# A decoder layer's last stretch: LayerNorm statistics as row sums on ScalarE, another order of the last products, norms in pieces

## The chip, the cores and the metric

The kernel runs on one core of one Trainium2 chip. Five engines work side by side, each through its own queue in order: TensorE (PE in the profile), VectorE (DVE), ScalarE (ACT), GpSimd (POOL) and SyncE (SP), which starts the transfers. They wait for one another through semaphores. The metric is the time of one execution on the device in microseconds (us); lower is better.

## The reference, cut to what matters

One layer over 1024 positions of width 1024, in float32. The change lies in the last two steps: the rest of the down product with LN2, and the gated embedding with LN3.

```python
def layer_norm(x, g, b):
    mu = jnp.mean(xf, axis=-1, keepdims=True)
    var = jnp.mean(jnp.square(xf - mu), axis=-1, keepdims=True)
    y = (xf - mu) * lax.rsqrt(var + LN_EPS)
    return (y * g + b)
...
h = jnp.square(jax.nn.relu(x @ w_up[i])) @ w_down[i]
x = layer_norm(DN_ALPHA * x + h, ln2_g[i], ln2_b[i])
ple = (p[i] @ w_ple[i]) * jax.nn.sigmoid(x @ w_ple_gate[i])
x = layer_norm(DN_ALPHA * x + ple, ln3_g[i], ln3_b[i])
```

## The kernel before

The 1024 positions are eight tiles of 128 rows (`xres[0]` to `xres[7]`, 128x1024 each, in SBUF). Every matrix product is three matmuls (`mm3`, lines 69 to 71): each float32 operand is split into a rounded high part and the low rest, and high x high, high x low and low x high are added in PSUM. ScalarE makes high parts (casts), VectorE or GpSimd low parts (a subtraction).

The down product runs in stages over the hidden width; each stage forms seven products p1 to p7 of half-size blocks (the seven-product scheme of Strassen's kind), each for four tiles t. One call `down(s, name, t)` (line 902) is one block: six matmuls into a PSUM bank, and one addition on VectorE out of that bank (`into`, line 890). Two chains share banks: p1, p6, p7, p4 go on in one bank per t, and p3 goes on in the bank in which p5 began, so a later block of a chain can start only when the addition of the block before it has read the bank. By `takers`, p5 of t goes to the right half of `xres[4+t]`, p3 to the right half of `xres[t]`, p7 and p4 to the right and left halves of `xres[4+t]`. So p3 of t is the last that `xres[t]` gets, and p4 of t the last for `xres[4+t]`.

In the last stage (line 1210 on) the order is `SEQ`: twelve blocks of p1, p2 and p6, then p5, p3, p7 and p4, four each. Beside them the next phase is prepared. The gate matrix is loaded in eight row blocks k; ScalarE casts the high part of each (line 1168), GpSimd subtracts for the low part (`gate_rest`, line 1158, 128x1024 each). `norm2(i)` is LN2 of tile i on VectorE: two `bn_stats` of 512 columns, `bn_aggr`, the addition of epsilon, the power -1/2 on GpSimd (line 103), and two passes over 128x1024 (lines 110 and 113). `turn2(i)` transposes a normed tile on TensorE (two PSUM banks of tag b0) and casts it; `rest2` subtracts its low part on VectorE.

Then comes the gate phase, one turn per tile i (line 1235): `gate` is 24 matmuls for each half of the columns (banks of tags b4 and b6, which the down product used for t = 2, 3 and t = 0, 1), a sigmoid on ScalarE and a product with the embedding on GpSimd; between the halves `turn2(i+1)`; then on VectorE LN3 of tile i-1, `rest2(i+1)`, LN2 of tile i+2 and two `merge` additions. The last tile goes in four quarters with the product on VectorE, and ends with its own LN3 and store.

What sets the order: under `manual_schedule` the named engines take instructions as the code is written. In the tail these are TensorE and VectorE, and GpSimd in a part of it; ScalarE and SyncE are ordered by a planner.

## Time and profile before

| what | value |
|---|---|
| median of 3 runs | 1250.26 us (1249.97 to 1251.74) |
| the profiled execution | 1249.6 us, of which span 1247.8 us |
| TensorE busy / weight loads | 94% / 78% of the span |
| VectorE, ScalarE, GpSimd busy | 75%, 45%, 43% |
| mean granted TensorE clock | 0.973 of full |

The span runs from the first to the last instruction of the profiled execution; the rest of its time lies around it. A stretch of the profile is read by what TensorE does in it: whether it is busy, at which granted clock (1.00 is 2.4 GHz, 0.50 is 1.2 GHz), and which engine ended its waits. A matmul's printed duration includes its pipeline, so the pace of TensorE is read from start to start. In this profile the last stage's p5 blocks begin at 1105 us, the first gate product at 1136.7, and TensorE's last matmul ends near 1239.9.

### The profile page before, as it was taken

Reading aid. Unit: us, or ns where it says so; the run is one execution under the profiler, and the core shown is the slowest. Engines: PE = TensorE matmul, PEld = TensorE weight load, DVE = VectorE, ACT = ScalarE, POOL = GpSimd, SP = SyncE. Lnnn points to the kernel's source line nnn. Section 1 sums busy time; section 2 is a strip of 40 time slices with the busy share of each in tenths; the row PEclk is TensorE's granted clock in tenths of the full one; section 3 lists DMA queues with packets and bytes.
Section 4 is the critical chain, followed back from the end, with each engine's and each line's share of the span. In section 5 each row is a group of like instructions: output and inputs, shape, how many; then the busy total and the mean of one; then the engine's idle time right before and its main releaser. Section 6 shows DMA issues by size and latency. Waiting matters only on the chain.

```text
span 1247.8 us, 15501 instructions
## 1 busy us (share of the span) xinstructions
PE 1169.4 (94%) x5520; PEld 967.2 (78%) x5520; DVE 939.1 (75%) x1169; ACT 558.1 (45%) x948; POOL 533.1 (43%) x368
## 2 busy tenths in 40 slices
PE   7999998899987998799899999999999999998997
PEld 5877777788866877688688888878888888876876
DVE  7745868796854678887577777688887888876998
ACT  5425756575644244455354554555433243421111
POOL 3212444454651336642334324257644456472432
PEclk9999999999997998899899999999999999998999
DMA  9824112121236373387788878899555665431121
GB/s 348 294 104 135 32 54 60 43 59 60 71 87 232 113 256 107 109 281 259 258 270 259 283 246 264 275 409 393 198 170 187 214 208 193 145 130 74 68 85 68
DMA packets 123580, 221.48 MB, mean 177 GB/s; under 512 B 9456, under 2 KB 64240, under 8 KB 123504
## 3 DMA queue, kind: packets, MB, share of 16 engines
q1 hardware_dynamic: 123504, 220.50, 52.3%
q8 instruction: 43, 0.70, 0.2%
q14 instruction: 33, 0.27, 0.1%
HBM read 148.12 MB, written 70.25 MB: 175 GB/s over the span
## 4 chain that ended last, share of the span: by engine, by line
PE 67%; DVE 12%; DMA 6%; issue 5%; ACT 5%; POOL 4%; SPq 1%; DVEq 0%; POOLq 0%; ACTq 0%
PE pd L69 7%; PE pd L70 7%; PE pd L71 7%; PE pu L71 6%; PE pu L70 6%; PE pu L69 6%; PE tp L126 3%; PE pq L69 3%; PE pq L70 2%; PE pq L71 2%; PE acc L70 2%; PE acc L69 2%; PE o L429 2%; PE acc L71 2%; DVE rr L400 2%
## 5 line engine op out<-in xcount | busy, mean ns | idle before, releaser
L890 DVE TENSOR_TENSOR xres<-xres,pd 128x512 f32<-128x512 f32 x208 | 137.0, 682 | 47.2 <-PE pd L71 46.6
L574 POOL TENSOR_TENSOR draw<-draw 128x512 f32<-128x512 f32 x64 | 97.9, 1530 | 174.0 <-DMA draw<-in_w_down_dram 171.3
L574 POOL TENSOR_TENSOR dop<-draw,dop 128x1024 fp32r<-128x1024 f32 (+1 forms) x48 | 112.5, 2362 | 127.3 <-ACT dop L866 121.2
L866 ACT CAST dop<-draw 128x1024 fp32r<-128x1024 f32 (+1 forms) x96 | 81.1, 905 | 135.8 <-PE pd L71 46.5
L69 PE MATMUL pd<-dop 128*128 128x512 f32 x320 | 125.5, 392 | 0.8 <-DVE xres L890 0.7
L70 PE MATMUL pd<-dop 128*128 128x512 f32 x320 | 124.9, 390 | 0.0
L71 PE MATMUL pd<-dop 128*128 128x512 f32 x320 | 124.7, 390 | 0.0
L103 POOL TENSOR_TENSOR rs<-var,mhalf 128x1 f32<-128x1 f32 x32 | 43.9, 1375 | 102.5 <-DVE var L101 95.9
L574 DVE TENSOR_TENSOR dop<-draw,dop 128x1024 fp32r<-128x1024 f32 (+1 forms) x48 | 85.7, 1786 | 2.5 <-ACT dop L866 2.5
L751 ACT COPY hid<-pu 128x512 f32<-128x512 f32 x48 | 28.3, 589 | 120.6 <-PE pu L71 68.3
L69 PE MATMUL pq<-xh,wh 128*128 128x512 f32 x192 | 78.2, 407 | 0.8 <-DVE ul L66 0.8
L400 DVE TENSOR_TENSOR_SCAN rr<-rr,diag 128x640 f32<-128x640 f32 (+3 forms) x32 | 71.4, 2232 | 8.2 <-ACT rr L398 8.1
L71 PE MATMUL pq<-xh,wl 128*128 128x512 f32 x192 | 76.6, 399 | 0.0
L70 PE MATMUL pq<-xl,wh 128*128 128x512 f32 x192 | 76.5, 399 | 0.0
L403 POOL TENSOR_TENSOR aa<-aa,rr 128x639 f32<-128x639 f32 (+3 forms) x32 | 56.9, 1780 | 44.9 <-DVE rr L400 44.9
L69 PEld LDWEIGHTS pd<-dop 128*128 128x128 f32 x320 | 60.4, 189 | 14.9 <-DVE xres L890 1.1
L70 PEld LDWEIGHTS pd<-dop 128*128 128x128 f32 x320 | 60.3, 189 | 12.6 <-POOL dop L574 0.3
L71 PEld LDWEIGHTS pd<-dop 128*128 128x128 f32 x320 | 60.2, 188 | 12.6
L574 DVE TENSOR_TENSOR hid<-pu,hid 128x512 f32<-128x512 f32 x48 | 33.0, 688 | 44.8 <-PE pu L71 36.8
L66 DVE TENSOR_TENSOR atl<-tp,ath 128x512 fp32r<-128x512 f32 (+2 forms) x96 | 50.8, 547 | 14.7 <-ACT ath L65 14.0
L65 ACT CAST wh<-wraw 128x1024 fp32r<-128x1024 f32 x36 | 38.0, 1057 | 51.2 <-PE acc L70 24.9
L70 PE MATMUL acc<-wl,mix 128*128 128x512 f32 x128 | 52.8, 412 | 2.4 <-POOL wl L66 2.4
(244 smaller groups left out, 3378.3 us busy)
## 6 DMA issues: line engine op xcount, KB each, us to landing
hspill<-hid SPq DMA_DIRECT2D x48, 512.0 KB, 5.0
draw<-hspill SPq DMA_DIRECT2D x48, 512.0 KB, 6.1
uraw<-in_w_up_dram SPq DMA_DIRECT2D x32, 512.0 KB, 6.3
draw<-in_w_down_dram SPq DMA_DIRECT2D x32, 512.0 KB, 4.5
tspill<-draw SPq DMA_DIRECT2D x64, 256.0 KB, 4.4
wraw<-in_w_out_dram SPq DMA_DIRECT2D x24, 512.0 KB, 3.6
draw<-in_w_down_dram SPq DMA_DIRECT2D x48, 256.0 KB, 5.1
wraw<-in_w_in_dram SPq DMA_DIRECT2D x16, 512.0 KB, 4.9
```

Source lines behind the costliest of these rows:

```text
L65: A.copy(out=h, in_=src)
L66: (eng or V).tensor_tensor(out=l, in0=src, in1=h.bitcast(F32), op=ALU.subtract)
L69: T.matmul(ps, lhsT=lh, rhs=rh, start=start, stop=False, **kw)
L70: T.matmul(ps, lhsT=lh, rhs=rl, start=False, stop=False, **kw)
L71: T.matmul(ps, lhsT=ll, rhs=rh, start=False, stop=stop, **kw)
L103: G.tensor_tensor(out=rs, in0=var, in1=mhalf[:, 0:1], op=ALU.pow)
L126: T.transpose(tp[:, j * P:(j + 1) * P], src[:, (k0 + j) * P:(k0 + j + 1) * P], ident)
L400: V.tensor_tensor_scan(out=rr[:, 0:n][:, ::-1], data0=rr[:, 0:n][:, ::-1], data1=diag[:, S - n:S][:, ::-1], initial=0.0, op0=ALU.mult, op1 ...
L403: G.tensor_tensor(out=aa[:, 0:n - 1], in0=aa[:, 0:n - 1], in1=rr[:, 1:n], op=ALU.mult)
L574: eng.tensor_tensor(out=o, in0=i0, in1=i1, op=op)
L866: A.copy(out=h, in_=raw)
L890: V.tensor_tensor(out=xres[i][:, cs], in0=xres[i][:, cs], in1=src, op=ALU.add)
```

## The change

- The statistics of LN2 and LN3 (all but the last tile's LN3) are taken on ScalarE (`act_stats`): a pass over the row with Identity and the sum along the row as a second output, a 128x1 step for minus the mean, a pass with Square and that as bias, again with its sum, and a 128x1 step for variance plus epsilon. GpSimd takes the power as before. The passes' own output goes to a tile that nothing reads (`unused`, one of the eight slots of tag X).
- The two passes of a norm on VectorE become `act_apply`, which adds minus the mean where `norm_apply` subtracted the mean. For tiles 0 and 1 they go in halves of 512 columns, one behind each addition of blocks 4 to 11.
- The order of the p5 and p3 blocks becomes p5 0, p5 1, p3 0, p5 2, p3 1, p5 3, p3 2, p3 3; p7 and p4 follow as before.
- `turn2(0)` stands behind p7 1, `rest2(0)` behind p4 0 and p4 1. In the gate phase LN2 of tile i+2 moves ahead of the second half of the gate, with the statistics of tile i+3 behind it; `rest2(i+1)` moves ahead of LN3 of tile i-1; the statistics of LN3 follow `merge`.
- The casts of the gate's blocks 4 to 7 are written among the blocks, and ScalarE's order is as written too.

```diff
--- before.py
+++ after.py
@@ -1157,23 +1157,47 @@
         h, l = gw[k]
         G.tensor_tensor(out=l, in0=graw[k], in1=h.bitcast(F32), op=ALU.subtract)
 
-    def gate_weights(k):
+    def gate_load(k):
+        graw.append(slot("ra" if k % 4 < 2 else "wr", "graw"))
+        load(graw[k], w_gate[k * P:(k + 1) * P, :])
+
+    def gate_high(k):
         if k < 4:
             gw.append((slot(next(tags), "gwh", F32R), slot(next(tags), "gwl", F32R)))
         else:
             both = big("gw")
             gw.append((both[:, 0:D], both[:, D:2 * D]))
-        graw.append(slot("ra" if k % 4 < 2 else "wr", "graw"))
-        load(graw[k], w_gate[k * P:(k + 1) * P, :])
         A.copy(out=gw[k][0], in_=graw[k])
 
     for k in range(4):
-        gate_weights(k)
+        gate_load(k)
+        gate_high(k)
         gate_rest(k)
     x2 = {}
 
-    def norm2(i):
-        layer_norm(xres[i], xres[i], g2, b2, "2")
+
+    lneps = const.tile([P, 1], F32, name="lneps")
+    V.memset(lneps, LN_EPS)
+    unused = []
+
+    def act_stats(i, tag):
+        s1, nm, s2, var, rs = [small.tile([P, 1], F32, name=nme, tag=nme + tag)
+                               for nme in ("s1", "nm", "s2", "va", "ra")]
+        A.activation(out=unused[0], in_=xres[i], func=AF.Identity, accum_out=s1)
+        A.activation(out=nm, in_=s1, func=AF.Identity, scale=-1.0 / D)
+        A.activation(out=unused[0], in_=xres[i], func=AF.Square, bias=nm, accum_out=s2)
+        A.activation(out=var, in_=s2, func=AF.Identity, scale=1.0 / D, bias=lneps)
+        G.tensor_tensor(out=rs, in0=var, in1=mhalf[:, 0:1], op=ALU.pow)
+        return nm, rs
+
+    def act_apply(i, stats, g, b, step, cs=slice(0, D)):
+        nm, rs = stats
+        if step == 0:
+            V.scalar_tensor_tensor(out=xres[i][:, cs], in0=xres[i][:, cs], scalar=nm,
+                                   in1=g[:, cs], op0=ALU.add, op1=ALU.mult)
+        else:
+            V.scalar_tensor_tensor(out=xres[i][:, cs], in0=xres[i][:, cs], scalar=rs,
+                                   in1=b[:, cs], op0=ALU.mult, op1=ALU.add)
 
     def turn2(i):
         both = big("x2")
@@ -1183,11 +1207,14 @@
             A.copy(out=x2[i][0][:, 4 * q:4 * q + 4, :], in_=tp)
         return tps
 
-    def rest2(i, tps):
-        for q, tp in enumerate(tps):
+    def rest2(i, tps, qs=(0, 1)):
+        for q in qs:
+            tp = tps[q]
             ks = slice(4 * q, 4 * q + 4)
             V.tensor_tensor(out=x2[i][1][:, ks, :], in0=tp, in1=x2[i][0].bitcast(F32)[:, ks, :],
                             op=ALU.subtract)
+
+    halves = (slice(0, CH), slice(CH, D))
 
     def gate(i, sg, pe, cs, c, eng):
         (xh2, xl2) = x2[i]
@@ -1205,50 +1232,67 @@
     def store(i, cs):
         load(out[i * P:(i + 1) * P, cs], xres[i][:, cs])
 
-    halves = (slice(0, CH), slice(CH, D))
     quarters = [slice(c, c + 256) for c in range(0, D, 256)]
-    with tc.manual_schedule(engines={mybir.EngineType.PE, mybir.EngineType.DVE}):
+    with tc.manual_schedule(engines={ET.PE, ET.DVE, ET.Activation}):
         for n, (name, t) in enumerate(SEQ[:12]):
             down(NS - 1, name, t)
             beside(NS - 1, n)
+        unused.append(big("unused").bitcast(F32)[:, 0:D])
         for k in range(4, NK):
-            gate_weights(k)
+            gate_load(k)
         g3 = load_rows("K", ln3_g[0], "g3")
         b3 = load_rows("K", ln3_b[0], "b3")
+
+        rest = [("p5", 0), ("p5", 1), ("p3", 0), ("p5", 2), ("p3", 1), ("p5", 3), ("p3", 2),
+                ("p3", 3)] + SEQ[20:]
+        st2, tps = {}, {}
+
+        def after(n):
+            if n in (2, 4):
+                st2[n // 2 - 1] = act_stats(n // 2 - 1, "2")
+            if n in (3, 5, 6, 7):
+                k = 4 if n == 3 else n
+                gate_high(k)
+                gate_rest(k)
+            if 4 <= n < 12:
+                i, m = (n - 4) // 4, (n - 4) % 4
+                act_apply(i, st2[i], g2, b2, m // 2, halves[m % 2])
+            if n == 9:
+                tps[0] = turn2(0)
+            if n in (12, 13):
+                rest2(0, tps[0], (n - 12,))
+
         with tc.manual_schedule(engines={mybir.EngineType.Pool}):
-            gate_rest(4)
-            gate_rest(5)
-            for name, t in SEQ[12:17]:
+            for n, (name, t) in enumerate(rest[:8]):
                 down(NS - 1, name, t)
-            norm2(0)
-            gate_rest(6)
-            for name, t in SEQ[17:24]:
-                down(NS - 1, name, t)
-            gate_rest(7)
-            tps = turn2(0)
-            rest2(0, tps)
-            for name, t in SEQ[24:26]:
-                down(NS - 1, name, t)
-            norm2(1)
-        for name, t in SEQ[26:]:
+                after(n)
+        for n, (name, t) in enumerate(rest[8:], 8):
             down(NS - 1, name, t)
+            after(n)
+        st2[2] = act_stats(2, "2")
+        st3 = {}
         for i in range(NT):
             last = i == NT - 1
             sg, pe = slot("K", "sg"), slot("K", "pe")
             load(pe, pspill[i])
             if not last:
                 gate(i, sg, pe, halves[0], 0, G)
-                tps = turn2(i + 1)
+                tps[i + 1] = turn2(i + 1)
+                if i + 2 < NT:
+                    for step in range(2):
+                        act_apply(i + 2, st2[i + 2], g2, b2, step)
+                if i + 3 < NT:
+                    st2[i + 3] = act_stats(i + 3, "2")
                 gate(i, sg, pe, halves[1], 1, G)
+                rest2(i + 1, tps[i + 1])
             if i:
-                layer_norm(xres[i - 1], xres[i - 1], g3, b3)
+                for step in range(2):
+                    act_apply(i - 1, st3[i - 1], g3, b3, step)
                 store(i - 1, slice(0, D))
             if not last:
-                rest2(i + 1, tps)
-                if i + 2 < NT:
-                    norm2(i + 2)
                 for cs in halves:
                     merge(i, sg, cs)
+                st3[i] = act_stats(i, "3")
         st = small.tile([P, 4, 6], F32, name="st", tag="st4")
         for c, cs in enumerate(quarters):
             gate(i, sg, pe, cs, c, V)
```

What this does to the engines' queues, at three places. A row is an instruction: line, operation, output and inputs with buffer numbers, size. First VectorE around the end of the p5 and p3 blocks. Before (pd is a PSUM bank of the down product, L97 to L113 norm 0):

```order
-L890 TENSOR_TENSOR xres7_7198<-xres7_7198,pd_9455 128x512
-L890 TENSOR_TENSOR xres0_7041<-xres0_7041,pd_9431 128x512
-L97 BN_STATS st_9470<-xres0_7041 128x6 x2
-L99 BN_AGGR mv_9473<-st_9470 128x2
-L101 TENSOR_SCALAR var_9475<-mv_9473 128x1
-L110 SCALAR_TENSOR_TENSOR xres0_7041<-xres0_7041,mv_9473,g2_9257 128x1024
-L113 SCALAR_TENSOR_TENSOR xres0_7041<-xres0_7041,rs_9477,b2_9259 128x1024
-L890 TENSOR_TENSOR xres1_7043<-xres1_7043,pd_9439 128x512
-L890 TENSOR_TENSOR xres2_7045<-xres2_7045,pd_9447 128x512
```

and with the change (nm is minus the mean, ra the power):

```order
+L890 TENSOR_TENSOR xres0_7041<-xres0_7041,pd_9424 128x512
+L890 TENSOR_TENSOR xres6_7196<-xres6_7196,pd_9457 128x512
+L890 TENSOR_TENSOR xres1_7043<-xres1_7043,pd_9432 128x512
+L1196 SCALAR_TENSOR_TENSOR xres0_7041<-xres0_7041,nm_9448,g2_9257 128x512
+L890 TENSOR_TENSOR xres7_7198<-xres7_7198,pd_9486 128x512
+L1196 SCALAR_TENSOR_TENSOR xres0_7041<-xres0_7041,nm_9448,g2_9257 128x512
+L890 TENSOR_TENSOR xres2_7045<-xres2_7045,pd_9457 128x512
+L1199 SCALAR_TENSOR_TENSOR xres0_7041<-xres0_7041,ra_9451,b2_9259 128x512
+L890 TENSOR_TENSOR xres3_7145<-xres3_7145,pd_9486 128x512
+L1199 SCALAR_TENSOR_TENSOR xres0_7041<-xres0_7041,ra_9451,b2_9259 128x512
+L890 TENSOR_TENSOR xres4_7192<-xres4_7192,pd_9289 128x512
```

The whole norm between the additions of p3 0 and p3 1 has become halves, one between each two additions. Second, GpSimd in the same stretch; before (gw are low parts of the gate matrix, L103 the power of a norm):

```order
-L1158 TENSOR_TENSOR gw_9407<-graw_9408,gw_9407 128x1024
-L1158 TENSOR_TENSOR gw_9411<-graw_9412,gw_9411 128x1024
-L103 TENSOR_TENSOR rs_9477<-var_9475,mhalf_74 128x1
-L1158 TENSOR_TENSOR gw_9415<-graw_9416,gw_9415 128x1024
-L1158 TENSOR_TENSOR gw_9419<-graw_9420,gw_9419 128x1024
-L103 TENSOR_TENSOR rs_9568<-var_9566,mhalf_74 128x1
```

and with the change:

```order
+L1190 TENSOR_TENSOR ra_9451<-va_9450,mhalf_74 128x1
+L1158 TENSOR_TENSOR gw_9465<-graw_9410,gw_9465 128x1024
+L1190 TENSOR_TENSOR ra_9479<-va_9478,mhalf_74 128x1
+L1158 TENSOR_TENSOR gw_9494<-graw_9412,gw_9494 128x1024
+L1158 TENSOR_TENSOR gw_9505<-graw_9414,gw_9505 128x1024
+L1158 TENSOR_TENSOR gw_9516<-graw_9416,gw_9516 128x1024
+L1190 TENSOR_TENSOR ra_9600<-va_9599,mhalf_74 128x1
```

The power of norm 0 now stands ahead of all four subtractions and that of norm 1 ahead of three. Third, ScalarE in a tile of the gate phase; before (sg is the sigmoid's output, x2 the turned tile):

```order
-L1198 ACTIVATE sg_9769<-pg_9772 128x512
-L1183 CAST x2_9799<-tp_9800 128x512
-L1183 CAST x2_9799<-tp_9805 128x512
-L1198 ACTIVATE sg_9769<-pg_9812 128x512
-L1198 ACTIVATE sg_9866<-pg_9869 128x512
```

and with the change (xres5 waits for LN2, xres2 for LN3):

```order
+L1225 ACTIVATE sg_9801<-pg_9804 128x512
+L1207 CAST x2_9831<-tp_9832 128x512
+L1207 CAST x2_9831<-tp_9837 128x512
+L1186 ACTIVATE unused_9409,s1_9846<-xres5_7194 128x1024
+L1187 ACTIVATE nm_9847<-s1_9846 128x1
+L1188 ACTIVATE unused_9409,s2_9848<-xres5_7194,nm_9847 128x1024
+L1189 ACTIVATE va_9849<-s2_9848,lneps_9285 128x1
+L1225 ACTIVATE sg_9801<-pg_9856 128x512
+L1186 ACTIVATE unused_9409,s1_9890<-xres2_7045 128x1024
+L1187 ACTIVATE nm_9891<-s1_9890 128x1
+L1188 ACTIVATE unused_9409,s2_9892<-xres2_7045,nm_9891 128x1024
+L1189 ACTIVATE va_9893<-s2_9892,lneps_9285 128x1
```

Behind each tile's casts there are now four instructions for LN2 of a later tile, and behind its second sigmoid four for its LN3. TensorE's rows are the same blocks and transposes in another order, SyncE's transfers stand as before, and no instruction ahead of the last stage's p5 blocks has moved but one 128x1 memset.

## Rows read from the trace of the kernel before

**Rows 1.** Timeline, TensorE (PE): start us, us, instruction, idle before it and what ended it.
```profile
1109.30 0.39 PE L69 MATMUL pd<-dop 128*128 128x512 f32 x1
...
1110.66 0.39 PE L69 MATMUL pd<-doph 128*128 128x512 f32 x1
...
1125.36 1.97 PE L126 MATMUL tp<-ident,xres 128*128 128x128 f32 x8 [3.65 <-DVE xres L890]
...
1136.73 0.77 PE L69 MATMUL pg<-gwh,x 128*128 128x512 f32 x1 [3.30 <-DVE xres L890]
...
1228.37 0.39 PE L71 MATMUL pg<-gwh,x 128*128 128x256 f32 x1 [0.51 <-DVE x L1189]
```

**Rows 2.** Stretches of the tail: busy us of each engine, granted clock (PEclk), DMA.
```profile
core 0: us, PE busy (x) PEld busy (x) DVE busy (x) ACT busy (x) POOL busy (x), PEclk, DMA share, GB/s
...
1125.30:1128.60 3.30, 3.25 (x12) 2.96 (x13) 3.30 (x6) 1.17 (x2) 1.02 (x1) 0.50 1.02 413
1136.70:1142.25 5.55, 5.52 (x13) 4.39 (x14) 0.48 (x1) 0.00 (x0) 0.00 (x0) 0.50 0.00 0
1156.85:1168.62 11.77, 11.77 (x58) 9.83 (x57) 10.82 (x14) 2.16 (x4) 4.88 (x4) 1.00 0.25 90
1193.09:1206.66 13.57, 12.33 (x56) 9.68 (x56) 12.55 (x17) 2.27 (x5) 5.49 (x4) 1.00 0.22 77
1220.19:1227.66 7.47, 6.58 (x34) 5.63 (x34) 6.96 (x10) 1.67 (x3) 2.71 (x2) 1.00 0.01 2
1227.66:1239.94 12.28, 11.73 (x96) 11.34 (x94) 10.70 (x20) 1.75 (x4) 2.75 (x2) 1.00 0.21 85
1239.94:1247.80 7.86, 0.00 (x0) 0.00 (x0) 4.34 (x9) 0.38 (x1) 0.92 (x1) 0.80 0.18 67
```

**Rows 3.** Timeline, VectorE (DVE).
```profile
1106.03 0.78 DVE L574 TENSOR_TENSOR dop<-draw,dop 128x512 fp32r<-128x512 f32 x1
...
1109.50 0.69 DVE L890 TENSOR_TENSOR xres<-xres,pd 128x512 f32<-128x512 f32 x1 [0.67 <-PE pd L71]
...
1114.45 3.46 DVE L110 SCALAR_TENSOR_TENSOR xres<-xres,mv,g 128x1024 f32<-128x1024 f32 x1
1120.72 3.38 DVE L113 SCALAR_TENSOR_TENSOR xres<-xres,rs,b 128x1024 f32<-128x1024 f32 x1 [2.81 <-POOL rs L103]
1124.03 4.26 DVE L890 TENSOR_TENSOR xres<-xres,pd 128x512 f32<-128x512 f32 x7
...
1240.36 0.43 DVE L1199 TENSOR_TENSOR sg<-sg,pe 128x256 f32<-128x256 f32 x1 [1.28 <-ACT sg L1198]
```

**Rows 4.** Timeline, GpSimd (POOL).
```profile
1103.34 2.91 POOL L1158 TENSOR_TENSOR gwl<-graw,gwh 128x1024 fp32r<-128x1024 f32 x1
...
1114.43 2.40 POOL L1158 TENSOR_TENSOR gw<-graw,gw 128x1024 fp32r<-128x1024 f32 x1 [2.72 <-ACT gw L1168]
...
1120.65 5.67 POOL L1158 TENSOR_TENSOR gw<-graw,gw 128x1024 fp32r<-128x1024 f32 x2
```

**Rows 5.** Groups by line, whole kernel: count | busy us, mean ns | idle before.
```profile
L97 DVE BATCH_NORM_STATS2 st<-xres 128x6 f32<-128x512 f32 x30 | 19.1, 677 | 0.0
...
L441 ACT ACTIVATE sq<-oraw 128x1024 f32<-128x1024 f32 x4 | 4.2, 1059 | 0.6 <-DVE oraw L436 0.5
...
L500 ACT COPY s<-y 128x1 f32<-128x1 f32 x4 | 0.8, 196 | 0.1
```

**Rows 6.** Timeline, ScalarE (ACT): the first sigmoid of the gate phase.
```profile
1145.05 0.60 ACT L1198 ACTIVATE sg<-pg 128x512 f32<-128x512 f32 x1 [17.10 <-PE pg L71]
```

**Rows 7.** Elsewhere: two gaps of TensorE, timeline rows, and the stretches behind them.
```profile
214.35 0.73 PE L429 MATMUL o<-atl,vs 128*128 128x128 f32 x4 [1.63 <-DVE atl L66]
...
285.18 1.17 PE L429 MATMUL o<-atl,vs 128*128 128x128 f32 x5 [2.28 <-DVE atl L66]
...
214.35:217.70 3.35, 3.35 (x19) 2.81 (x19) 3.26 (x4) 2.52 (x6) 1.43 (x3) 1.00 0.00 0
285.52:288.93 3.41, 3.41 (x16) 3.31 (x16) 2.02 (x4) 1.31 (x4) 0.41 (x1) 0.50 0.53 155
```

## The prediction

> **What bounds the kernel now.** I read the table of stretches first, then TensorE's timeline, then those of the engines that it waits for. Up to 1105 us TensorE runs its blocks without a break, six matmuls in 1.36 us (1109.30 to 1110.66, [rows 1]). The tail that the change rewrites is different. TensorE stands still twice, 3.65 us ahead of the first transposes and 3.30 us ahead of the first gate product, both times put down to an addition of VectorE [rows 1], and behind each gap the granted clock is 0.50, the lower level (1.2 GHz), for 1125.30 to 1128.60 and 1136.70 to 1142.25 [rows 2]. The additions were late because they stand behind whole norms in VectorE's queue: the first pass of norm 0 took 3.46 us and the second 3.38 us, after which seven additions ran in one go [rows 3]. In the gate phase the pitch from one tile's first sigmoid to the next one's is 11.77 us early on, with TensorE busy throughout, and 13.57 us later, where TensorE is busy for 12.33 and VectorE for 12.55 of it [rows 2]: there VectorE sets the pace.
>
> What would TensorE alone need? From the start of block p5 0 (1105.22, four blocks ahead of 1110.66, [rows 1]): 16 blocks x 1.36 = 21.76 and eight transposes. A tile's 48 matmuls take 10.88 (48 x 1.36 / 6) of the undisturbed pitch of 11.77 [rows 2], so transposes cost 0.89. The gate would start at 1127.87, not 1136.73: 8.86 us. Its first half takes 5.44 + 0.15 to the sigmoid, not 8.32 (1136.73 to 1145.05, [rows 1, 6]): 2.73 us. From 1145.05 to 1220.19 lie six pitches, 75.14, against 6 x 11.77 = 70.62: 4.52 us. From there to the next sigmoid are 7.47 [rows 2], against 6.36 in the first tile (half a tile, the transposes and 0.03): 1.11 us. The next stretch of 12.28 [rows 2] holds a wait of 0.51 for VectorE [rows 1]. Sum 17.73 us; a tail that TensorE alone paces ends at a span of 1230.1.
>
> **The change, part by part.**
>
> *Statistics to ScalarE.* Each of 15 norms loses two bn_stats of 0.68 us on VectorE [rows 5] and two small operations, some 1.7 us. ScalarE gets two passes over 128x1024 and two 128x1 steps. Nearest rows: a Square of that size 1.06, a 128x1 copy 0.20 [rows 5]. So 1.06 + 0.20 + 1.06 + 0.20, about 2.5 us. No row here has a sum along the row: its reading could be free or cost another small instruction, 0 to 0.3 us per pass; I take 0.1 for the sum and keep both ends. It can't cost less than the same pass without it. No extra table load stands in the new order. ScalarE per gate tile: 2 x 2.7 + 2 sigmoids (0.60 each, [rows 6]) + 2 casts of about the same = 7.8 of 11.77 us. Hidden.
>
> *The gate phase.* VectorE per tile: four passes of a norm over 128x1024 (two times 0.60 each, by the pitch in [rows 3]), two low parts and two merges of 0.60, 7.2 us; and two 128x512 products on GpSimd can hold it up, half a subtraction's 2.40 each [rows 4]: 9.6. TensorE paces at 11.77, and the 4.52 + 1.11 + 0.51 of this phase are saved: 6.14. The last tile: the statistics of tile 6 end about 1 us later than with bn_stats, but VectorE waited 1.28 us for the last sigmoid [rows 3], of which 0.5 go with TensorE's wait; 0 to 0.4 us, I take 0. The 7.86 us behind TensorE's end [rows 2] stay.
>
> *p3 of tile t behind p5 of tile t+1, norms in halves.* The row of tile 0 is now complete in block 3 (the addition at 1109.50, [rows 3]), two blocks before. ScalarE's sums follow at 1110.2, both passes are through at 1112.8, the power on GpSimd at 1114. With nothing in the way its four halves alternate with additions, norm 0 is done at 1117.6, behind the addition of p3 3, and the transposes at 1118.8 (ten blocks behind 1105.22) find it ready.
>
> *What is in the way.* GpSimd subtracts the low parts of four gate weights in this very stretch: the first followed ScalarE's cast at 1114.43 [rows 4], and the change leaves load and cast where they were, with the powers of the two norms between. When a subtraction of GpSimd and a VectorE instruction with two SBUF inputs meet, the second waits for the whole of the first: the subtraction from 1114.43 took 2.40 and the norm pass of 1114.45 ended 1.08 after it; of the two subtractions from 1120.65 the first let the norm pass wait until 1123.0 (its end at 1124.1 less 1.08), and the second waited for that end (5.67 for both, [rows 3, 4]); and a 128x512 subtraction on VectorE at 1106.03 ended 0.56 after GpSimd's at 1106.25 [rows 3, 4]. Additions out of PSUM don't wait: seven ran at a pitch of 0.60 beside it [rows 3]. So they take turns, and a half of a norm (0.56 us of work) can wait for 2.25 us of subtraction. Halves don't help there: each half can meet a subtraction of its own.
>
> VectorE from 1112.2 on, to the addition of p4 2, whose PSUM bank the gate needs: 11 additions and 2 low parts x 0.60 = 7.8; 8 halves x 0.6 = 4.8; 4 subtractions x 2.25 = 9.0, in each of which one addition gets done (4 x 0.60), so 6.6 of waiting. End 1131.4, with 0.3 us for steps between engines 1131.7. The gate starts at 1131.8, not 1127.87: 3.9 us back. If the first turn goes the other way (the power and the second subtraction reach GpSimd 0.1 us ahead of VectorE's last half of norm 0) the transposes wait 2.3 us, and the end is 1132.2: the same sum in another place.
>
> The Trainium skill, "SBUF — State Buffer", Who interferes with whom, says that the shared port pair is an exclusive lock for a whole instruction and takes VectorE only with two SBUF inputs. Traces agree (0.60 against 3.46). By a port that is shared in proportion, as one might think, the 3.9 us would be near 0: that is the second rival below.
>
> *The clock.* The wait ahead of the gate splits: block p4 3 waits for the addition of p7 3 (VectorE reaches it five steps of 0.6 ahead of p4 2's end, at 1128.0), where TensorE would have begun it at 1126.5: 1.5 us; then the gate waits from 1129.5 to 1131.8, 2.3 us. Behind a gap of 2.28 us elsewhere in this trace the clock was 0.50 for 3.41 us; behind one of 1.63 us it stayed at 1.00 [rows 7]. At half clock 3.41 us do 1.7 us of work. The gap here is nearest to 2.28, so I count 1.7 us, with 0 and 2.8 (the second gap of before) as ends.
>
> **Sum.** 17.73 - 3.9 - 1.7 = 12.1 us off the span of 1247.8 (the profiled run itself took 1249.6, the median of the three is 1250.26): 1250.26 - 12.1 = 1238.2.
>
> **Rivals.**
> 1. Turns as above, but the gap falls where it is hidden or stays short, no lower clock: 1236.5. For it: the order of two events 0.1 us apart decides where the gap lies, and VectorE's lag, not TensorE, sets the gate's start in both. Against it: the 2.3 us come out in most readings.
> 2. No turns of weight, the subtractions slip in where VectorE adds: 1250.26 - 17.7 = 1232.5. For it: the halves were cut for that. Against it: all the meetings in [rows 3, 4].
> 3. More is lost: a lower clock at the transposes and another at the gate (1.7), sums that cost 0.3 us a pass (0.5 to the gate's start), and 0.2 us a tile on the gate's pitch (1.4): 12.1 less 3.6 is 8.5, so 1241.8. For it: the gaps leave little room between them.
> 4. Slower than before: the sum along the row makes a pass of ScalarE long. Its place is the gate phase, where ScalarE has four passes a tile. Per tile it needs 4p + 3.2 us; it overtakes TensorE's 11.77 at p = 2.1, and the whole gain of 12.1 is gone when seven tiles lose 1.73 each, at p = 2.6. At p = 3 the tile takes 15.2, seven lose 24, and the time is 1262. Against it: 1.06 in [rows 5], and no row suggests 2.5 times that. The Trainium skill, "ScalarE: Activation LUTs", Rules for kernel authors, points to this side: it wants adds and multiplies on VectorE, as faster per element. The trace agrees on the speed (1.36 us for two bn_stats against two passes of 1.06) and not on the end, since up to p = 2.1 the longer passes lie beside TensorE's work.
>
> That the change doesn't do what it says is excluded by the order: the statistics are on ScalarE and the blocks stand as written; what remains of it is rival 3.
>
> **Chances.** Forecast 0.48, rival 1 0.23, rival 2 0.10, rival 3 0.16, rival 4 0.03. The range runs from just above rival 2 to rival 3: 1233 to 1242. A measurement tells about 0.2% (2.5 us) from no change; all but rival 4 and the worst of rival 3 are faster: faster 0.94, same 0.03, slower 0.03.
>
> **What the profile after should show.** ScalarE's passes at 1.05 to 1.35 us. VectorE's halves at 0.7 and, four or so of them, near 2.3 us beside GpSimd's subtractions, until the gate starts; gaps of TensorE of 1.5 and 2.3 us (or 2.3 at the transposes) and a lower clock of 3.4 us behind the larger; the gate from 1131.8 or 1132.2; a pitch of 11.77 from the first sigmoid to the seventh, with no wait of TensorE; 7.9 us behind its end. It would be wrong if halves are short and TensorE has no gap (rival 2), if passes are much over 1.35 (rivals 3, 4), or if the pitch stays above 12, which would mean that something other than bn_stats paces VectorE there.

## The result, and the profile after

The changed kernel takes 1238.67 us (median of seven runs, 1234.35 to 1244.77) against 1250.26 (1245.72 to 1251.74): a ratio of 0.9918, 95% interval 0.9901 to 0.9935. The prediction was 1238.2 in 1233 to 1242. A second batch gave 1236.69 against 1248.95, ratio 0.9900 (0.9880 to 0.9919).

TensorE's timeline of the changed kernel, around the last block and the first gate product:

```profile
1130.65 0.50 PE L69 MATMUL pd<-dop 128*128 128x512 f32 x1 [1.13 <-DVE xres L890]
...
1131.92 0.39 PE L71 MATMUL pd<-dop 128*128 128x512 f32 x1
...
1134.40 0.47 PE L69 MATMUL pg<-gwh,x 128*128 128x512 f32 x1 [2.09 <-DVE xres L890]
```

Of the two gaps of 3.65 and 3.30 us in [rows 1] these 1.13 and 2.09 are left, ahead of the last block and of the gate; the transposes (at 1121.38) no longer wait. The stretches, which answer to [rows 2]:

```profile
core 0: us, PE busy (x) PEld busy (x) DVE busy (x) ACT busy (x) POOL busy (x), PEclk, DMA share, GB/s
1107.77:1129.50 21.73, 21.73 (x99) 17.46 (x97) 18.82 (x20) 15.43 (x26) 18.65 (x10) 1.00 0.47 157
1129.50:1134.40 4.90, 1.68 (x8) 1.08 (x7) 4.90 (x9) 0.00 (x0) 0.91 (x1) 1.00 0.65 265
1134.40:1140.14 5.74, 5.74 (x26) 4.72 (x27) 2.93 (x3) 0.00 (x0) 0.00 (x0) 1.00 0.00 0
...
1163.90:1175.67 11.77, 11.77 (x59) 9.83 (x57) 7.54 (x8) 7.72 (x17) 3.91 (x4) 1.00 0.25 89
...
1228.72:1236.72 8.00, 0.00 (x0) 0.00 (x0) 4.87 (x11) 0.38 (x1) 0.99 (x1) 0.68 0.17 66
```

In 1129.50 to 1134.40 VectorE has no idle moment: it is what TensorE waits for. The gate's first half ran at clock 1.00; a late tile takes 11.77 us with TensorE busy throughout and VectorE for 7.54 of it. VectorE and GpSimd ahead of the gate (compare [rows 3, 4]):

```profile
1115.47 0.75 DVE L1196 SCALAR_TENSOR_TENSOR xres<-xres,nm,g 128x512 f32<-128x512 f32 x1
...
1118.10 2.21 DVE L1199 SCALAR_TENSOR_TENSOR xres<-xres,ra,b 128x512 f32<-128x512 f32 x1
1120.23 0.67 DVE L890 TENSOR_TENSOR xres<-xres,pd 128x512 f32<-128x512 f32 x1
1120.82 0.74 DVE L1199 SCALAR_TENSOR_TENSOR xres<-xres,ra,b 128x512 f32<-128x512 f32 x1
...
1122.08 2.29 DVE L1196 SCALAR_TENSOR_TENSOR xres<-xres,nm,g 128x512 f32<-128x512 f32 x1
...
1124.90 2.30 DVE L1196 SCALAR_TENSOR_TENSOR xres<-xres,nm,g 128x512 f32<-128x512 f32 x1
...
1127.72 2.28 DVE L1199 SCALAR_TENSOR_TENSOR xres<-xres,ra,b 128x512 f32<-128x512 f32 x1
```

```profile
1117.07 2.68 POOL L1158 TENSOR_TENSOR gw<-graw,gw 128x1024 fp32r<-128x1024 f32 x1 [0.45 <-ACT gw L1170]
...
1120.91 8.54 POOL L1158 TENSOR_TENSOR gw<-graw,gw 128x1024 fp32r<-128x1024 f32 x3 [0.20 <-ACT gw L1170]
```

Of the eight halves four took 0.74 or 0.75 us and four 2.21 to 2.30, each of these beside one of the four subtractions; additions out of PSUM stay at 0.67 to 0.69. On ScalarE one norm's statistics read:

```profile
1112.77 1.06 ACT L1186 ACTIVATE unused<-xres 128x1024 f32<-128x1024 f32 x1 [0.68 <-DVE xres L890]
1113.74 0.18 ACT L1186 ACTIVATION_READ_ACCUMULATOR unused<-xres 128x1 f32 x1
1113.95 0.20 ACT L1187 ACTIVATE nm<-s 128x1 f32<-128x1 f32 x1
1114.19 1.15 ACT L1188 ACTIVATE unused<-xres,nm 128x1024 f32<-128x1024 f32 x1
1115.25 0.19 ACT L1188 ACTIVATION_READ_ACCUMULATOR unused<-xres,nm 128x1 f32 x1
1115.47 0.29 ACT L1189 ACTIVATE va<-s,lneps 128x1 f32<-128x1 f32 x1
```

The first pass is as long as the one in [rows 5], the second, with the mean as its bias, takes 1.15 us; each sum is read out by an instruction of its own, 0.18 and 0.19 us. From first to last it is 2.99 us.

### The profile page after: what moved, and what is told of

Same layout as the page of the kernel before. It is cut to its first block, busy times and chain, and to the rows that moved or that the text cites. A ratio compares the mean times of both kernels' runs of the same rounds, so it can differ in the third digit from the quotient of the medians.

```text
span 1236.7 us, 15529 instructions
## 1 busy us (share of the span) xinstructions
PE 1163.7 (94%) x5520; PEld 964.1 (78%) x5520; DVE 903.1 (73%) x1114; ACT 599.2 (48%) x1038; POOL 520.3 (42%) x368
## 4 chain that ended last, share of the span: by engine, by line
PE 71%; DVE 10%; ACT 6%; DMA 5%; issue 5%; POOL 2%; SPq 1%; DVEq 0%; ACTq 0%; POOLq 0%
PE pd L69 8%; PE pd L71 7%; PE pd L70 7%; PE pu L70 6%; PE pu L71 6%; PE pu L69 6%; PE tp L126 3%; PE pq L69 3%; PE pq L70 3%; PE pq L71 2%; PE acc L70 2%; PE o L429 2%; DVE rr L400 2%; PE acc L71 2%; PE acc L69 2%
## 5 line engine op out<-in xcount | busy, mean ns | idle before, releaser
L71 PE MATMUL pd<-dop 128*128 128x512 f32 x320 | 124.6, 389 | 0.0
L574 DVE TENSOR_TENSOR hid<-hid,hid 128x512 f32<-128x512 f32 x48 | 53.8, 1145 | 0.6
```

The costliest lines, as they stand in the source:

```text
L71: T.matmul(ps, lhsT=ll, rhs=rh, start=False, stop=stop, **kw)
L574: eng.tensor_tensor(out=o, in0=i0, in1=i1, op=op)
```

## All runs in one table

Every profile's tail, read from the timelines: from the start of block p5 0 to the first gate product (A), from there to the first sigmoid (B), six pitches to the seventh tile's first sigmoid (C), on to the last sigmoid (D), and to the end (E); all in us. p5 0 itself began between 1102.5 and 1109.2 in these fourteen profiles, 1105.22 in before, 1107.77 and 1104.35 in the two of the changed kernel, though nothing ahead of it was edited but one 128x1 memset: that much a single time hangs on the execution. The sum A to E is free of it. The ratio is that of the times to before in the same batch, with its 95% interval; before's median was 1250.26 in the first, 1248.95 for e0 to e3, 1249.62 for e4, e5, e7 and e8, and 1250.11 for e6, e9, e10 and e11.

| kernel | A | B | C | D | E | sum | median | ratio |
|---|---|---|---|---|---|---|---|---|
| before | 31.51 | 8.31 | 75.13 | 19.75 | 7.84 | 142.6 | 1250.26 | |
| changed | 26.62 | 5.75 | 70.97 | 17.60 | 8.00 | 128.9 | 1238.67 | 0.9918 (0.9901 to 0.9935) |
| e0 changed, again | 27.22 | 5.76 | 70.98 | 17.60 | 8.01 | 129.6 | 1236.69 | 0.9900 (0.9880 to 0.9919) |
| e1 blocks only | 26.62 | 7.36 | 75.13 | 19.76 | 7.84 | 136.7 | 1245.42 | 0.9973 (0.9958 to 0.9988) |
| e2 gate phase only | 32.07 | 7.11 | 70.88 | 17.61 | 8.44 | 136.1 | 1242.57 | 0.9948 (0.9932 to 0.9963) |
| e3 two turns fewer | 25.25 | 5.77 | 70.97 | 17.63 | 8.00 | 127.6 | 1236.34 | 0.9898 (0.9880 to 0.9915) |
| e4 whole norms | 23.94 | 5.76 | 70.97 | 17.60 | 8.01 | 126.3 | 1234.54 | 0.9879 (0.9860 to 0.9897) |
| e5 gate sums on VectorE | 26.62 | 7.38 | 70.62 | 17.83 | 7.82 | 130.3 | 1234.99 | 0.9882 (0.9866 to 0.9898) |
| e6 one more pass | 27.12 | 7.35 | 72.87 | 15.70 | 9.48 | 132.5 | 1239.95 | 0.9921 (0.9890 to 0.9953) |
| e7 two more passes | 27.12 | 7.34 | 84.67 | 14.33 | 11.80 | 145.3 | 1253.74 | 1.0034 (1.0017 to 1.0050) |
| e8 norm 1 later | 22.69 | 5.64 | 70.98 | 17.60 | 8.02 | 124.9 | 1233.19 | 0.9864 (0.9849 to 0.9879) |
| e9 old VectorE order | 27.10 | 7.34 | 74.63 | 15.99 | 7.96 | 133.0 | 1240.62 | 0.9917 (0.9893 to 0.9941) |
| e10 no sums on ScalarE | 29.53 | 5.64 | 70.74 | 17.84 | 7.85 | 131.6 | 1238.88 | 0.9911 (0.9888 to 0.9935) |
| e11 e8 with e5 | 22.65 | 5.64 | 70.62 | 17.83 | 7.81 | 124.6 | 1229.12 | 0.9835 (0.9809 to 0.9860) |

C and D are read at sigmoids. In e6, e7 and e9 a sigmoid stands behind sums in ScalarE's queue and starts after its product is ready, which lengthens C and shortens D. What the gate phase costs is then C + D: 94.88 in before, 88.57 in the changed kernel, 88.45 in e5, 88.57 in e6, 99.00 in e7 and 90.62 in e9.

## The experiments

**The change again, and its two parts.** The theory: the blocks' part and the gate phase's part add up.

> The changed kernel once more, unedited. In its first profile the gate's first product started 26.63 us behind the start of block p5 0 (31.51 before), with gaps of 1.13 and 2.09 us ahead of it and the clock at 1.00 behind both. If turns between VectorE and GpSimd set that start, it comes again at 26.3 to 27.0 us and VectorE's norm halves show about four of 2.2 to 2.3 us. On the clock: if a gap of 2.1 us is followed by the lower clock in some executions and not in others, this profile may show 3.4 us at 0.50 in the gate's first half, which then takes 7.4 us to its sigmoid in place of 5.74; if the lower clock needs a longer gap, 5.74 again. Time 1236 to 1241 us.

In e0 A is 27.22, with gaps of 1.79 us ahead of the second half of the transposes and 1.97 ahead of the gate, and halves of 2.20, 2.90, 2.28 and 2.29 us. It is the other order of turns that the prediction named (a wait at the transposes), and A lies 0.2 us above the range expected here. B is 5.76 again.

> Only the last 16 blocks as changed (p3 behind p5, statistics of norms 0 and 1 on ScalarE, halves, gate weights); the gate phase in its old order with bn_stats on VectorE. If the two parts of the gain lie one behind the other and simply add, the gate starts 26.6 us behind the start of p5 0 (4.9 us earlier than before), its first half saves 2.6 more, the later pitch is 13.6 us as before, and the time is 1250.3 - 7.5 = 1242.8 us (1244.5 with a lower clock behind the gap). Rival: VectorE comes later into the gate phase with its old queue, and what the blocks gain is given back there: 1247 us or more, with waits of TensorE from the second tile on.

```diff
-        st2[2] = act_stats(2, "2")
...
-                    for step in range(2):
-                        act_apply(i - 1, st3[i - 1], g3, b3, step)
+                    layer_norm(xres[i - 1], xres[i - 1], g3, b3)
...
+                    norm2(i + 2)
```

A is that of the changed kernel (26.62), C, D and E are those of before to 0.01 us: the parts don't touch each other. The batch's medians differ by 3.5 us, less than the 5.9 of the two tails; the two spans by 2.7 (1247.8 and 1245.1), since p5 0 began 3.2 us later in this profile. Behind its gap of 2.08 us the clock was lower for 3.40 us:

```profile
1132.95:1135.03 2.08, 0.00 (x0) 0.03 (x1) 2.08 (x5) 0.00 (x0) 0.00 (x0) 1.00 0.18 71
1135.80:1139.20 3.40, 3.40 (x9) 2.63 (x8) 0.00 (x0) 0.00 (x0) 0.00 (x0) 0.50 0.00 0
```

> Only the gate phase as changed (statistics of its norms on ScalarE, its new order); the 16 blocks before it and norms 0 and 1 as before. If the parts add, the gate starts 31.5 us behind the start of p5 0 as before, with the lower clock behind its gap, the pitch is 11.8 us for all tiles, and the time is 1250.3 - 6.1 = 1244.2 us. Rival: the pitch of the gate phase is set by how late VectorE enters it, and without the changed blocks the first tiles still wait for VectorE: 1247 us or more.

In e2 lines 1218 to 1234 of before stand in place of the new blocks (with `tps` as a dictionary), and the gate loop is the changed one. C fell by 4.25 us and D by 2.14, as in the changed kernel; the batch's medians differ by 6.4. The tails of e1 and e2 gain 5.9 and 6.5 us, 12.4 together, with the lower clock in e1; those of the changed kernel gain 13.6 and 13.0.

**The turns.** The theory: four subtractions of GpSimd, each of which lets one norm half wait, are the whole delay of the gate. Call it a meeting when a subtraction and a norm pass are due at the same time; each of these kernels moves the meetings.

> The changed kernel with the casts and low parts of gate weights 4 to 7 behind the casts of tile 0's transposes, so that GpSimd's four subtractions meet at most one norm half. If turns between VectorE and GpSimd cost the 3.9 us that the prediction took for them, halves last 0.75 us but for one, the gate starts 23.1 us behind the start of p5 0 in place of 26.6, with no gap of TensorE over 0.6 us, and the time is 3.5 us below the changed kernel's in the same batch (5.2 below an execution of it with the lower clock): 1235 us. Rival: VectorE is late for another reason (additions, the powers, ScalarE's chain): the same time as the changed kernel's, within 1 us. Second rival: the subtractions come too late for the gate's fifth step (they have about 1 us): TensorE waits inside the gate's first half and the gain is under 2 us.

```diff
-            if n in (3, 5, 6, 7):
-                k = 4 if n == 3 else n
-                gate_high(k)
-                gate_rest(k)
...
             if n == 9:
                 tps[0] = turn2(0)
+                for k in range(4, NK):
+                    gate_high(k)
+                    gate_rest(k)
...
```

Two halves still met the subtractions, one more than I had counted. VectorE, then GpSimd, in e3:

```profile
1122.05 2.64 DVE L1199 SCALAR_TENSOR_TENSOR xres<-xres,ra,b 128x512 f32<-128x512 f32 x1
1124.61 0.68 DVE L890 TENSOR_TENSOR xres<-xres,pd 128x512 f32<-128x512 f32 x1
1125.21 2.31 DVE L1199 SCALAR_TENSOR_TENSOR xres<-xres,ra,b 128x512 f32<-128x512 f32 x1
```

```profile
1121.73 10.35 POOL L1158 TENSOR_TENSOR gw<-graw,gw 128x1024 fp32r<-128x1024 f32 x4 [4.84 <-ACT gw L1170]
```

A is 25.25 instead of 23.1, and the gain of 1.3 to 2 us in the tail is too small to be seen in the times (0.9898 against 0.9900). Halves that met nothing ran at TensorE's own pace, one and an addition in 1.36 us, the time of a block:

```profile
1117.83 0.69 DVE L890 TENSOR_TENSOR xres<-xres,pd 128x512 f32<-128x512 f32 x1
1118.44 0.75 DVE L1196 SCALAR_TENSOR_TENSOR xres<-xres,nm,g 128x512 f32<-128x512 f32 x1
1119.19 0.69 DVE L890 TENSOR_TENSOR xres<-xres,pd 128x512 f32<-128x512 f32 x1
```

So the halves in themselves don't delay the gate. Whether the meetings are the whole delay this run leaves open; the next two bear on it.

> The changed kernel with norms 0 and 1 applied in whole passes of 128x1024 (one behind every second block) in place of halves; all else as changed. If VectorE and GpSimd take turns, what is lost is the subtractions' time, whatever the passes' length: four passes that each can wait for one subtraction lose as much as eight halves, and the gate starts within 1 us of 26.6 to 27.2 us behind the start of p5 0 (the two profiles of the changed kernel), same time within 1.5 us. Rival: cutting the norms into halves is what lets additions through in time; with whole passes of 3.4 us the gate starts 2 us or more later, 28.6 to 31 us, and the time is 2 to 4 us above.

```diff
-                act_apply(i, st2[i], g2, b2, m // 2, halves[m % 2])
+                if m in (1, 3):
+                    act_apply(i, st2[i], g2, b2, m // 2)
```

Both the theory's number and the rival fell: whole passes are better, A is 23.94. VectorE's four passes in e4:

```profile
1115.48 1.28 DVE L1196 SCALAR_TENSOR_TENSOR xres<-xres,nm,g 128x1024 f32<-128x1024 f32 x1
...
1118.20 1.91 DVE L1199 SCALAR_TENSOR_TENSOR xres<-xres,ra,b 128x1024 f32<-128x1024 f32 x1
1120.04 1.27 DVE L890 TENSOR_TENSOR xres<-xres,pd 128x512 f32<-128x512 f32 x2
1121.23 2.74 DVE L1196 SCALAR_TENSOR_TENSOR xres<-xres,nm,g 128x1024 f32<-128x1024 f32 x1
1123.90 1.27 DVE L890 TENSOR_TENSOR xres<-xres,pd 128x512 f32<-128x512 f32 x2
1125.09 2.23 DVE L1199 SCALAR_TENSOR_TENSOR xres<-xres,ra,b 128x1024 f32<-128x1024 f32 x1
```

Three meetings cost 0.63 + 1.46 + 0.95 = 3.0 us over the free 1.28; the four halves of the changed kernel cost 2.21 + 2.29 + 2.30 + 2.28 less 4 x 0.75, 6.1 us: 1.0 us a meeting against 1.5. As the lines read, there are fewer meetings, and two additions stand between two passes (1120.04, 1123.90) and go on beside the subtraction, where one stands between two halves.

> The changed kernel with tile 1's norm applied behind the last block's addition (its transposes come half a gate tile later) and all four gate-weight casts and subtractions behind the sums of norm 1, so that GpSimd's 9 us of subtractions run where VectorE only adds out of PSUM. If turns are the whole delay of the gate's start: no VectorE instruction over 0.8 us between the casts and the gate but perhaps one of 1.5, no gap of TensorE over 0.4 us, the gate 22.7 to 23.2 us behind the start of p5 0 (26.6 and 27.2 in the changed kernel, 25.25 in the run with two turns left), and the time 3.5 to 4.5 us below the changed kernel's 1236.7: 1232.5 us. Rival: something else holds VectorE (additions, or a bank) and the gate comes at 25 us again; the time stays within 1 us of 1236.5. Second rival: the norm passes moved behind the blocks meet the subtractions there and tile 1's transposes wait in the gate's first tile: the gain is given back there as a gap ahead of those transposes.

```diff
-            if n in (3, 5, 6, 7):
-                k = 4 if n == 3 else n
-                gate_high(k)
-                gate_rest(k)
-            if 4 <= n < 12:
...
+            if n == 4:
+                for k in range(4, NK):
+                    gate_high(k)
+                    gate_rest(k)
+            if 4 <= n < 8:
+                act_apply(0, st2[0], g2, b2, (n - 4) // 2, halves[n % 2])
+            if n == 15:
+                for step in range(2):
+                    act_apply(1, st2[1], g2, b2, step)
```

```profile
1104.60:1127.29 22.69, 22.69 (x106) 18.85 (x104) 15.53 (x23) 15.33 (x26) 17.61 (x10) 1.00 0.49 167
```

```profile
1116.49 9.90 POOL L1158 TENSOR_TENSOR gw<-graw,gw 128x1024 fp32r<-128x1024 f32 x4 [0.39 <-ACT gw L1170]
```

TensorE is busy for all of the 22.69 us, there is no gap, and the four subtractions take 9.90 us beside additions of 0.69. With no meeting the whole delay is gone. This run also takes norm 1's four halves out of the blocks, 3.0 us of work on VectorE; by e3 halves that meet nothing delay nothing there. Over the 22.65 that the prediction took for TensorE alone the gate is late by 0.04 us with no meeting, 1.29 with three of whole passes, 2.60 with two of halves, 3.97 and 4.57 with four. The Trainium skill, "SBUF — State Buffer", Who interferes with whom, calls the port pair that VectorE and GpSimd share an exclusive lock for a whole instruction. It lets VectorE take that pair with two SBUF inputs and also in its 2-port modes, which the prediction left out. These rows agree: additions with one input in PSUM stayed at 0.69 beside the subtractions. Moving norm 1 was free, since its transposes come only half a tile into the gate phase.

**What holds the gate phase's pitch.** My theory: bn_stats on VectorE made 13.57 us, ScalarE's sums give 11.77.

> The changed kernel with the statistics of the 13 norms of the gate phase back on VectorE (bn_stats, bn_aggr and two 128x1 steps) at the same places of the new order; norms 0 and 1 stay on ScalarE. If the statistics' 1.7 us per norm are what paces the late tiles, VectorE has 7.54 + 3.4 = 10.9 us of work and some 1 to 2 us of waiting for GpSimd per tile: the pitch of the late tiles is 12.5 to 13.6 us, TensorE waits from the fourth or fifth tile on, and the time is 4 to 6 us above the changed kernel's 1236.7: 1241 to 1243 us. Rival: the new order alone takes the waits away, the pitch stays at 11.8 and the time within 1 us of the changed kernel's.

```diff
+    def vec_stats(i, tag):
+        st = small.tile([P, 2, 6], F32, name="vst", tag="vst" + tag)
+        for h in range(2):
+            V.bn_stats(out=st[:, h, :], in_=xres[i][:, h * CH:(h + 1) * CH])
...
-                st3[i] = act_stats(i, "3")
+                st3[i] = vec_stats(i, "3")
```

The theory fell: with bn_stats in the new order the pitch is 11.77 for all six tiles, and the time the same as the changed kernel's or better (0.9882 against 0.9918 and 0.9900). A late tile of before, VectorE and then GpSimd:

```profile
1196.62 1.28 DVE L110 SCALAR_TENSOR_TENSOR xres<-xres,mv,g 128x1024 f32<-128x1024 f32 x1
1198.34 2.31 DVE L113 SCALAR_TENSOR_TENSOR xres<-xres,rs,b 128x1024 f32<-128x1024 f32 x1 [0.44 <-POOL rs L103]
```

```profile
1196.78 1.52 POOL L103 TENSOR_TENSOR rs<-var,mhalf 128x1 f32<-128x1 f32 x1 [4.00 <-DVE var L101]
1198.27 1.29 POOL L1199 TENSOR_TENSOR sg<-sg,pe 128x512 f32<-128x512 f32 x1
```

The power (0.55 us when alone) is asked for just as the first pass begins, waits for it and takes 1.52; VectorE waits for the power; and GpSimd's product, next in its queue, gets its turn ahead of the second pass, which takes 2.31 in place of 1.28. That is 0.44 + 1.03 us, twice in a tile: 2.9 us. By estimate VectorE's round without them is 13.57 - 2.9 = 10.6 us, under TensorE's 11.77. The same tile part in e5, and e5's stretch:

```profile
1175.46 1.28 DVE L1227 TENSOR_TENSOR x<-tp,x 128x512 fp32r<-128x512 f32 x2
1176.65 1.28 DVE L1209 SCALAR_TENSOR_TENSOR xres<-xres,vnm,g 128x1024 f32<-128x1024 f32 x1
1178.04 1.28 DVE L1212 SCALAR_TENSOR_TENSOR xres<-xres,vra,b 128x1024 f32<-128x1024 f32 x1
1179.24 2.38 DVE L1242 SCALAR_TENSOR_TENSOR xres<-xres,sg 128x512 f32<-128x512 f32 x2
```

```profile
1159.00:1170.77 11.77, 11.77 (x58) 9.83 (x57) 11.53 (x18) 2.17 (x4) 5.54 (x4) 1.00 0.24 85
```

Between statistics and passes stands other work now, so the power is there in time and the passes are free; one turn is left, at the merges (2.38 us for two). VectorE is busy for 11.53 of 11.77: it fits, barely. That these turns and waits are what the order removes is read from the lines; no run takes away them alone.

> The changed kernel with VectorE's old order of a gate tile (norm of the tile before, low parts, norm of the tile after next, merges) and the sums on ScalarE. The run with bn_stats in the new order showed that the order alone holds 11.77 us. If ScalarE's sums alone do so too (VectorE has 7.5 us of work a tile, and each norm's second pass may still wait for GpSimd's product, 1 us twice), the pitch is 11.8 us as in the changed kernel and the time within 1 us of 1236.7. Rival: the order is what the pitch hangs on, and late tiles need 12.5 us or more: 1240 us or more.

```diff
-                if i + 2 < NT:
-                    for step in range(2):
-                        act_apply(i + 2, st2[i + 2], g2, b2, step)
...
-                rest2(i + 1, tps[i + 1])
...
             if not last:
+                rest2(i + 1, tps[i + 1])
+                if i + 2 < NT:
+                    for step in range(2):
+                        act_apply(i + 2, st2[i + 2], g2, b2, step)
                 for cs in halves:
                     merge(i, sg, cs)
```

The rival came true: late pitches of 12.6 us. But C + D is 90.62, 4.26 below before, of the changed kernel's 6.31: TensorE waits only for 0.50, 0.48 and 0.21 us, in the last tiles. ScalarE and then VectorE in e9:

```profile
1190.69 1.06 ACT L1186 ACTIVATE unused<-xres 128x1024 f32<-128x1024 f32 x1 [4.71 <-DVE xres L1229]
```

```profile
1193.38 1.28 DVE L1196 SCALAR_TENSOR_TENSOR xres<-xres,nm,g 128x1024 f32<-128x1024 f32 x1 [2.73 <-ACT unused L1188]
1195.11 2.31 DVE L1199 SCALAR_TENSOR_TENSOR xres<-xres,ra,b 128x1024 f32<-128x1024 f32 x1 [0.45 <-POOL ra L1190]
```

The sums wait for the merges, which are VectorE's last work of a tile, and the norm that waits for the sums is its first work of the next: 9.38 us of work + 2.73 + 0.45 of waiting = 12.6. So the order holds the pitch with either engine's statistics; ScalarE's sums alone bring it from 13.6 to 12.6 us, not to TensorE's 11.77.

> The order of the changed kernel everywhere, but all statistics on VectorE by bn_stats, those of norms 0 and 1 in the 16 blocks too. If VectorE paces these blocks (its work and its turns were 26.6 us there), two norms' statistics of 1.8 us each come on top and the gate starts 29 to 30.5 us behind the start of p5 0; the gate phase keeps its 11.77 us; the time is 3 to 4 us above the run with bn_stats in the gate phase alone (1235.0): 1238 to 1239 us. Rival: the statistics fill places where VectorE waits for a block anyway, and the earlier casts move the turns: gate at 26 to 27.5 us, 1235 us, and ScalarE's sums would be worth nothing.

Here `vec_stats` stands in the blocks too. A is 29.53 against 26.62, as VectorE paces these blocks. The four subtractions all met halves of norm 0 here, which took 2.25 to 2.78 us, and the transposes waited for it: the 2.9 us are what the sums on ScalarE are worth together with the place of the turns.

**How near ScalarE is to pacing.** Extra sum passes in `act_stats` of the gate phase; their sums go nowhere.

```diff
+        for _ in range(more):
+            s0 = small.tile([P, 1], F32, name="s0", tag="s0" + tag)
+            A.activation(out=unused[0], in_=xres[i], func=AF.Identity, accum_out=s0)
```

> The changed kernel with two further sum passes of 128x1024 on ScalarE ahead of each norm's mean in the gate phase (their sums are not used), four more per tile: 4 x 1.25 = 5.0 us. ScalarE then has 7.72 + 5.0 = 12.7 us of work per tile against TensorE's 11.77. If ScalarE lies hidden up to TensorE's pitch and paces beyond it, the pitch is 12.7 to 12.9 us, five to six tiles lose 1 us each, and with the last tile's sums 2.5 us later the time is 6 to 8 us above the changed kernel's: 1243 to 1245 us. Rival: ScalarE's chain is on the path already (statistics to apply to transposes), and each tile loses most of the 5.0 us: 1260 us or more. Rival on the other side: the order has room for it, below 1240 us.

> The changed kernel with one further sum pass of 128x1024 on ScalarE ahead of each norm's mean in the gate phase (its sum is not used), two more per tile, 1.21 us each with its reading. By work alone ScalarE has 7.72 + 2.4 = 10.1 us per tile, under TensorE's 11.77: the pitch stays at 11.8 and the time within 1.5 us of the changed kernel's 1236.7. By the loop that the run with two more passes showed (12.01 us of work and 2.15 us of waiting for VectorE's second merge, with the next sigmoid queued behind the sums: pitch 14.48), the pitch is 14.48 - 2.42 = 12.06 us, with TensorE waiting for the bank ahead of each tile's first half: about 0.3 us a tile and 1.2 in the last tile's sums, 1239 to 1241 us.

With two more the pitch is 14.48 us, not 12.8, though ScalarE works for only 12.01 of it. ScalarE in e7, second sigmoid, first of LN3's passes, next sigmoid, and a wait of TensorE:

```profile
1189.75 0.58 ACT L1228 ACTIVATE sg<-pg 128x512 f32<-128x512 f32 x1
1192.48 1.06 ACT L1186 ACTIVATE unused<-xres 128x1024 f32<-128x1024 f32 x1 [2.15 <-DVE xres L1232]
...
1197.60 0.58 ACT L1228 ACTIVATE sg<-pg 128x512 f32<-128x512 f32 x1
```

```profile
1184.24 0.50 PE L69 MATMUL pg<-gwh,x 128*128 128x512 f32 x1 [2.10 <-ACT x L1210]
```

LN3's sums wait 2.15 us for product and merge, and behind them stand the next sigmoid and the casts of the turned tile, for which TensorE waits. ScalarE's round is its work, this wait and 0.3 us of steps between instructions. e6 bears the round out: 12.1 us, where work alone gives 10.1. It doesn't bear out the loss per tile that was expected from it. TensorE in e6 is busy throughout, from the second transposes to the seventh:

```profile
1152.34:1211.31 58.97, 58.97 (x282) 49.19 (x280) 36.23 (x38) 44.05 (x90) 17.93 (x19) 1.00 0.26 89
```

The sigmoids fall behind by 0.3 us a tile, six tiles don't use up TensorE's lead, and C + D is the changed kernel's 88.57. What the pass costs lies in E, 9.48 us for 8.00, where the last norm but one waits for its sums; the time is in the expected range only with the lower clock in B (1.6 us):

```profile
1224.72 1.29 DVE L1199 SCALAR_TENSOR_TENSOR xres<-xres,nm,g 128x1024 f32<-128x1024 f32 x1 [3.77 <-ACT unused L1191]
```

**The two best together.**

> The best two together: norm 1 applied behind the blocks and the subtractions behind its sums (gate at 22.69 us, no gap), and bn_stats on VectorE in the gate phase. If both hold, the tail from block p5 0 is 22.7 + 5.75 + six pitches of 11.77 + 17.7 + 7.8 = 124.6 us against 124.9 with the sums on ScalarE, the same time within 1 us: 1233 us. Rival: VectorE now enters the gate phase with norm 1 and the statistics of tile 2 still to do, and with 11.5 us of work per tile of 11.77 it can't catch up: waits of TensorE ahead of the first tiles' transposes, 1235 us or more.

`act_stats` becomes `vec_stats` in the gate phase of e8. Six pitches of 11.77, no gap of TensorE from p5 0 to its end, 1229.12 us: 1.65% (1.40 to 1.91) below before and the best of all. Its tail is 0.3 us shorter than e8's, and p5 0 began 2.0 us earlier in its profile (1102.62 and 1104.60); the rest of the 4 us between the two medians, taken in two batches, the profiles don't show.

## Why the prediction was right, and where it wasn't

- **What TensorE alone needs** (17.73 us): right. e8 and e11 reach A of 22.69 and 22.65, and e11's tail of 124.6 is within 0.3 us of the prediction's 1230.1 less 1105.22.
- **The turns** (3.9 us): right in mechanism, place and size: 3.97 and 4.57 us late. The gate came at 1131.85 in the time of before (1134.40 less the 2.55 us by which p5 0 began later), forecast 1131.8; gaps of 1.13 and 2.09 against 1.5 and 2.3. (Between the additions of p7 3 and p4 2 lie six steps of 0.6 us, not five; six give the 1128.0 that the prediction uses, and 1128.04 was measured.) "Halves don't help there" was too mild: they make it worse (e4). That a port shared in proportion would cost near 0 was not worked out; shared evenly it would make a half of 0.75 us at most 1.5, by estimate, and 2.20 to 2.90 were measured.
- **The clock** (1.7 us): it didn't come. Rival 1's branch is in both profiles of the changed kernel, B 5.75 and 5.76. The term has the right size where it occurs (7.34 to 7.38 in five kernels with the same gap, 1.6 us more).
- **The gate phase** (4.52 + 1.11 + 0.51 = 6.14): 4.16 in C and 2.15 in D, 6.31. The size was right and the cause wrong. The step that failed is "VectorE per tile": it took the bn_stats that leave VectorE as the gain. e5 shows that the order alone gives all of it (C + D 88.45), and e9 that the move without the order gives 4.26 of the 6.31.
- **Statistics on ScalarE**: 0.1 us for reading a sum, measured 0.18 to 0.21. It cost nothing: VectorE, not ScalarE's chain, was late at the gate.
- **Rival 4**: its break point of p = 2.1 us counted ScalarE's work without its wait. From 14.48 and 12.1 us, a round without extra passes is 9.7; 2.07 us are left, 0.5 for each of four passes, and ScalarE's round passes 11.77 near p = 1.8, by estimate. Seven tiles then don't yet lose time: in e6, past that point, C + D stayed.
- **The last tile** (0 to 0.4): E grew by 0.16 us.
- **The total** fits better than its steps, and that is in part luck: the tail gained 13.6 and 13.0 us in the two profiles, not 12.1, and p5 0 began 2.55 us later in the first. The second batch's 1236.69 lies at rival 1's 1236.5.
- **Open**: no run keeps the old order of p5 and p3 with the rest of the change, so what that order is worth by itself isn't shown.

## What to carry to other kernels

Where two engines take turns on a resource, count meetings, not bytes: cutting an instruction into pieces can raise the number of meetings, and moving one side to where the other engine reads only PSUM beside it removes them. Ahead of taking work off an engine that seems to pace, look whether it is busy with work or with turns and short waits inside its order; other work put between a statistic and its use was worth more (6.4 us of C + D) than the move by itself (4.3). An engine's spare time is its pitch less its work and less what it waits for in order, since what stands behind that wait is late too.

## What the runs showed of the hardware

- A sum along the row costs ScalarE a second instruction, ACTIVATION_READ_ACCUMULATOR, 0.18 to 0.21 us; Square with a bias from SBUF took 1.15 us where the pass without took 1.06.
- The same gap isn't always followed by the lower clock. Ahead of the gate, gaps of 1.97 to 2.09 us were followed by 0.50 for some 3.4 us in five profiles (e1, e5, e6, e7, e9) and by 1.00 in two (the changed kernel's), and one of 2.44 us (e3) by 1.00. Within e7 three gaps of 2.10 to 2.14 us were followed twice by 1.00 and once by 0.50 (1214.30 to 1217.70). What else decides these runs leave open.
- A 128x1 power on GpSimd takes 0.55 us alone and, in the tail, up to 1.54 (e3) beside a norm pass of VectorE: small operations take turns as well.
